# A fifth half-unit of weights in the opening block of each stage

## The chip, the cores and the metric

The kernel runs on one core of one Trainium2 chip. The metric is the device time of one execution in microseconds (us); a kernel's figure is the median of its runs. In the profile PE is TensorE (matmul), PEld its weight loads, DVE is VectorE, ACT is ScalarE, POOL is GpSimd and SP is SyncE, which issues the DMAs.

## What the kernel computes

Two layers act on 256 latent tokens and 256 context tokens of width 1024, with shared weights. Each layer is a half-step SwiGLU FFN, a mixing block, and a second half-step FFN. The core of the reference:

```python
for i in range(DEPTH):
    last = i == DEPTH - 1
    h = ffn_half_step(h, g_ffn1[i], m[0], m[1], m[2], w13_ffn1[i], w2_ffn1[i])
    hc = ffn_half_step(hc, g_ffn1[i], mc[0], mc[1], mc[2], w13_ffn1[i], w2_ffn1[i])
    n_lat = modulate(rms_norm(h, g_mix[i]), m[3], m[4])
    n_ctx = modulate(rms_norm(hc, g_mix[i]), mc[3], mc[4])
    z = n_lat @ w_in[i]
    zc = n_ctx @ (w_in[i][:, OFF_KV:OFF_G] if last else w_in[i])
    ...
    h = h + m[5] * y
    h = ffn_half_step(h, g_ffn2[i], m[6], m[7], m[8], w13_ffn2[i], w2_ffn2[i])
    if not last:
        ...                       # the same for hc
return rms_norm(h, g_final)
```

`ffn_half_step` is `h + 0.5 * gate * swiglu(modulate(rms_norm(h)))`. In the last layer the context is only needed for keys and values, so the last mixing block and the last FFN work mostly on the latent tokens alone.

## The kernel before, in words

**Data.** Activations lie feature-major: 8 chunks of 128 features by 512 columns, of which the first 256 are the latent tokens (half 0) and the next 256 the context tokens (half 1). Every float32 product is made of three matmuls in a reduced format (`mm3`, lines 191 to 193): high part of the weights times high part of the operand (`whi`, `nhi`), high times low (`whi`, `nlo`), and low times high (`wlo`, `nhi`).

**Weights.** They come as half-units: 128 output features by all 1024 inputs, 512 KB each. SP loads them in a fixed order into five staging tiles (`stg`). A conversion (`conv`, line 298) turns a staged half-unit into a pair of tiles: ScalarE copies the high part (`whi`, line 157) and then VectorE subtracts for the low part (`wlo`, line 165). For the second, third and fourth half-unit of each stage (the set `on_pool`) GpSimd makes the low part instead (line 303). There are five pairs (`HI = 5`). A half-unit that is finished (`done`, line 316) asks for the conversion of the one four places on (`AHEAD = 4`), so that at the opening of a stage four half-units are converted or under way and the fifth is not asked for until the first of the four is finished.

**Order.** A planner (`Weaver`) holds an estimate of TensorE's time. Side tasks (conversions, norms, evacuations) are generators that give the time at which they are next due; whenever the estimate passes a due time the task is resumed and emits its next instructions. This fixes the order on each engine's queue when the program is written. On the chip every engine works through its queue in that order and waits on semaphores.

**Changes of stage.** A stage ends with eight M-tiles in `final_half`, the last four of them half by half, latent half first. The norm of each half follows: sums of squares (ScalarE `sq`, GpSimd `acc`), a chain over TensorE, GpSimd and VectorE for the factor, and then `apply` (line 544) per chunk: `nt` on VectorE, `nhi` on ScalarE, `nlo` on VectorE. The next stage opens with `gemm_start` (line 604): four half-units, half by half, with the chunks k outermost and half-units in pairs (0, 1) and (2, 3), so that TensorE can start on chunk 0 while later chunks are still being normed.

`gemm_start` opens five stages: the first mixing block (stage M0, at 409 us of the span), the second FFN of layer 0 (F0, 573), the first FFN of layer 1 (F1, 946), the second mixing block (M1, 1322) and the last FFN (FL, 1419). It also opens the output projection inside each mixing block, which is not changed. FL is special ("raw"): the norm's factor is applied behind the product, and the operand of chunk k comes straight from the residual (`raw_in`, line 537). In M1 only half-units 2 and 3 have a context half; in FL none has.

**After the opening.** In an FFN the fifth half-unit is the first of the third pair (`pa`), made by `gemm` over all 512 columns. In a mixing block it is half of the gating input `u`, made by `gemm(i0 + 4, vs)`; after it come four (in M1 two) blocks of the gating input `vg` (lines 1309 to 1311), which use the sixth half-unit for chunks 0 to 3 and the seventh for chunks 4 to 7. When pair (2, 3) is done in a mixing block, `ev_kv` and `q_task` put the key, value and query work on VectorE and ScalarE.

Of the kernel before, what the change touches and what calls it, by code (L numbers as in the profile page):

```python
# [19 lines left out]
D = 1024  # L20
# [11 lines left out]

# columns of the per-layer parameter packs
PK1 = {}
# [19 lines left out]
class Weaver:  # L54
    """Keeps an estimate of TensorE's time and resumes side tasks when their turn comes."""

# [48 lines left out]
class Slots:  # L105
    """A fixed set of equal tiles, handed out in the order in which they came back."""

# [21 lines left out]
def block_kernel(ctx: ExitStack, tc: tile.TileContext, ins, out: bass.AP):  # L129
# [10 lines left out]

    # ---------------------------------------------------------------- pools
    cst = ctx.enter_context(tc.tile_pool(name="cst", bufs=1))
# [11 lines left out]

    # ---------------------------------------------------------------- engine helpers
    def act(o, i, func, after=0.0, n=None, **kw):
# [42 lines left out]

    # ---------------------------------------------------------------- the weight stream  # L200
    loads = []
# [121 lines left out]

    # ---------------------------------------------------------------- constants and residual
    ident = cst.tile([P, P], F32, name="ident")
# [40 lines left out]

    # ---------------------------------------------------------------- modulation
    mods, gains, gates, n_ada, n_mod = {}, {}, {}, {}, {}
# [14 lines left out]
    def gain_from(l, i, c0=0, c1=KC, n=2):  # L383
        """A = sqrt(D) g (1 + scale) for norm i."""
        m = mods[l][:, :n, (1, 4, 7)[i] * 8 + c0:(1, 4, 7)[i] * 8 + c1]
        vstt(gains[l][:, i, :n, c0:c1], m, 1.0,
             gains[l, "g"][:, i, None, c0:c1].to_broadcast([P, n, c1 - c0]), ALU.add, ALU.mult)
# [16 lines left out]
    def ada_quarter(q, tiles):  # L404
        """Layer 0's m0 and m1, column chunks 2q and 2q+1."""
        ps = yield from SM.get()
# [23 lines left out]
    def ada_tile(j, l, i):  # L430
        """128 columns of the modulation: VectorE's dot products of w_ada's columns with silu(c)."""
        r, c = i // KC, i % KC
# [20 lines left out]

    # ---------------------------------------------------------------- norms
    last = [False]
    acc, acc_i, acc_n, acc_t, last_sq = {}, {}, {}, {}, {}

    def square_in(v, c):
        """Adds the squares of h's chunk c, half v, to half v's sum."""
        if v not in acc:  # L460
# [19 lines left out]
    def sum_of(v):  # L480
        """Waits for half v's sum of squares; gives it with the time it is there."""
        while acc_n.get(v, 0) < KC:
            yield W.t + 50.0
        yield acc_t[v]
        acc_n[v] = 0
        return [acc.pop(v)] + ([last_sq.pop(v)] if v in last_sq else [])

    def rstd_chain(srcs, nblk, n_feat):
        """1/sqrt(sum + n eps) of the columns of src [128, 128 nblk], broadcast over partitions (in PSUM)."""
        ps = yield from SM.get()  # L490
        for b in range(nblk):
            for n, src in enumerate(srcs):
                t1 = mm(ps[:, b:b + 1], src[:, P * b:P * b + P], ones[:, :1], n == 0, n == len(srcs) - 1)
        yield from rstd_tail(ps, t1, nblk, n_feat)
        return ps
# [26 lines left out]

    # The last norm's factors are applied behind the first products: these take A h with the shift as one more column.
    raw_done = set()
# [19 lines left out]
    def apply(l, i, v, R, c0=0, c1=KC):  # L544
        """The modulated norm of h's chunks c0..c1, half v, as an exact sum of two float32r parts."""
        prev = None
# [28 lines left out]

    # ---------------------------------------------------------------- GEMM pieces
    hi_ = [0]
# [9 lines left out]
    def cols(ps, vs):  # L587
        """The columns of a PSUM tile that hold the halves vs."""
        return ps[:, vs[0] * T:(vs[-1] + 1) * T]

    def gemm(i, vs, nk=KC, xs=None, ps=None, ok=None, raw=False):
        """A feature-major tile: half-unit i against all k, halves vs."""
        ps = ps or ps_new()
# [10 lines left out]
    def gemm_start(i0, vss, evacs, ks=range(KC), ok=None, raw=False):  # L604
        """The four half-units at i0, half by half, k outermost, behind what makes their operand."""
        ok = ok or (lambda v, k: n_done.get(v, 0) > k)
        for j in range(4):
            conv_upto(i0 + j)
        pss = [ps_new() for _ in range(4)]
        for v in (0, 1):  # L610
            groups = [((0, 1), ks), ((2, 3), ks)]
            if not raw and 1 not in vss[3]:
                groups = [((0, 1, 2, 3), ks[:-2]), ((0, 1), ks[-2:]), ((2, 3), ks[-2:])]
            for js, k_part in groups:
                js = [j for j in js if v in vss[j]]
                if js:
                    for k in k_part:
                        W.until(lambda: ok(v, k))
                        xh, xl = raw_of(k) if raw else n_of(k, v)
                        for j in js:  # L620
                            wh, wl = wk(i0 + j, k)
                            mm3(pss[j][:, :T + 2] if raw else cols(pss[j], [v]), wh, wl, xh, xl, k == ks[0], k == ks[-1])
                for u in ((0, 1), (2, 3)):
                    if js and js[-1] == u[1] and k_part[-1] == ks[-1]:
                        if v == max(max(vss[u[0]]), max(vss[u[1]])):
                            for j in u:
                                done(i0 + j)
                            W.spawn(evacs[u[0] // 2](pss[u[0]], pss[u[1]]), W.t + 200.0)

    # ---------------------------------------------------------------- FFN  # L630
    def ffn(l, which, vs, tail):
        """h += 0.5 m (silu(a) b) w2 with a, b from the norm's output. Ends with the squares of the new h."""
        i_norm = (0, 2)[which - 1]
        full = len(vs) == 2
        with tc.tile_pool(name="ffn%d%d" % (l, which), bufs=2) as fp:
# [50 lines left out]
            for pi, (k0, k1_) in enumerate(PARTS):  # L686
# [3 lines left out]
                for m in range(k0, k1_):  # L690
# [3 lines left out]
                    if m == 0:  # L694
# [7 lines left out]
                        else:  # L702
                            gemm_start(i0, [vs] * 4, [evac(0, raw), evac(1, raw)],
                                       ok=(lambda v, k: k in raw_done) if raw else None, raw=raw)
                        hi_[0] += 4
# [43 lines left out]
    def final_half(vs, nk, xs, upd, tail, ok, raw=None):  # L749
        """The last eight M-tiles: the second four half by half, with h's squares and the norms behind them."""  # L750
        if xs:
# [29 lines left out]
    def fill():  # L781
        """Starts the modulation's tiles whose turn has come."""
        while ada_next[0] < len(ada_at):
# [15 lines left out]

    # ---------------------------------------------------------------- start  # L800
    def start_units(i0, evacs, fp, ST, GT):
        """The modulation's first columns, the first norm and the first half-units, in the order of arrival."""
        n_units = HI
# [47 lines left out]
        def chain(v):  # L851
            """The norm's factors of half v."""
            t = []
# [77 lines left out]

    # ---------------------------------------------------------------- mixing
    def mixing(l, tail):
# [4 lines left out]
        with ExitStack() as es:  # L938
# [23 lines left out]

            # -- blockdiag(C_c w_f), blockdiag(-S_c w_f)
            def bd_task():
# [13 lines left out]

            # -- q, k, v
            tb = Slots(W, mp, "tb", [P, 512], F32, TB)  # L980
# [106 lines left out]

            # -- attention
            def scores(v, hd, qb, pt):
                """exp of the scores, normalised and transposed into pt, for one block of queries."""  # L1090
                k0 = 0 if v == 0 else T
# [32 lines left out]
            def attention(v):  # L1124
                """All heads of half v's queries."""
                k0 = 0 if v == 0 else T
# [37 lines left out]

            # -- gating
            def y_of(g, j, v):
# [43 lines left out]

            # -- Fourier
            def fourier(v):
# [37 lines left out]

            # -- pooling
            def pooling(v):
# [30 lines left out]

            # -- the stream of projections
            gemm_start(i0, [vs, vs, [0, 1], [0, 1]], [ev_q, ev_kv])
            ps = gemm(i0 + 4, vs)
            done(i0 + 4)

# [54 lines left out]

    # ---------------------------------------------------------------- the two layers
    def norm_next(l, i):
# [34 lines left out]

# [1 line left out]
def _tiles(w):  # L1382
    """[K, M] -> [M/128, 128 (k in chunk), K/128, 128 (m)]"""
    k, m = w.shape
# [38 lines left out]
def _half_swap(w):  # L1423
    """Swaps the two halves of each rope axis in the last 32 columns' axis."""
    s = w.shape[:-1]
# [88 lines left out]
```

## Time and profile before

| | |
|---|---|
| median of 3 runs | 1625.59 us (1624.21 to 1625.91) |
| span of the profiled execution | 1622.2 us |
| granted TensorE clock, mean | 0.997 of full speed |
| TensorE busy | 1583.4 us, 98% of the span |
| VectorE busy | 1020.5 us, 63% |
| ScalarE busy | 556.9 us, 34% |
| GpSimd busy | 145.2 us, 9% |
| DMA | 245.53 MB, mean 151 GB/s |

The profile shows one execution. Its span goes from its first to its last instruction; the profile gives no other time for this execution, and the median of the runs is 3.4 us more than the span. Matmuls are pipelined and their ends are modelled, so that two matmuls overlap in the rows; time lost on TensorE is best read from start to start. An idle time in square brackets is followed by what ended it.

### The profile page before, as it was taken

Reading aid. Unit: us, or ns where it says so; the run is one execution under the profiler, and the core shown is the slowest. Engines: PE = TensorE matmul, PEld = TensorE weight load, DVE = VectorE, ACT = ScalarE, POOL = GpSimd, SP = SyncE. Lnnn points to the kernel's source line nnn. Section 1 sums busy time; section 2 is a strip of 40 time slices with the busy share of each in tenths; the row PEclk is TensorE's granted clock in tenths of the full one; section 3 lists DMA queues with packets and bytes.
Section 4 is the critical chain, followed back from the end, with each engine's and each line's share of the span. In section 5 each row is a group of like instructions: output and inputs, shape, how many; then the busy total and the mean of one; then the engine's idle time right before and its main releaser. Section 6 shows DMA issues by size and latency. Waiting matters only on the chain.

```text
span 1622.2 us, 22411 instructions
## 1 busy us (share of the span) xinstructions
PE 1583.4 (98%) x8862; PEld 1339.3 (83%) x8862; DVE 1020.5 (63%) x1693; ACT 556.9 (34%) x845; POOL 145.2 (9%) x115
## 2 busy tenths in 40 slices
PE   5999999999999999999999999999999999999997
PEld 3788888888867998888888898888888887899997
DVE  4568777877757476465563366776464367776674
ACT  3332221233534352222222243222222245554443
POOL 2000000004211320000000130000000051220001
PEclk9999999999999999999999999999999999999999
DMA  9355655654211144343352225566463222255452
GB/s 355 144 188 195 195 191 172 225 181 166 88 44 53 54 180 156 127 156 136 124 168 95 87 74 178 177 209 232 169 222 136 84 103 93 88 191 183 166 200 72
DMA packets 72057, 245.53 MB, mean 151 GB/s; under 512 B 8336, under 2 KB 10640, under 8 KB 71184
## 3 DMA queue, kind: packets, MB, share of 16 engines
q1 hardware_dynamic: 71664, 243.71, 44.0%
q8 instruction: 69, 1.13, 0.3%
q10 hardware_dynamic: 288, 0.39, 0.1%
q14 instruction: 36, 0.29, 0.1%
HBM read 243.03 MB, written 1.05 MB: 150 GB/s over the span
## 4 chain that ended last, share of the span: by engine, by line
PE 93%; DVE 5%; ACT 1%; issue 1%; DMA 0%; POOL 0%; SPq 0%; DVEq 0%; ACTq 0%; POOLq 0%
PE mm L191 28%; PE mm L193 28%; PE mm L192 28%; PE mm L184 5%; DVE nlo L169 2%; PE mm L197 1%; PE mm L1325 1%; PE mm L410 1%; DVE nt L169 1%; PE mm L1326 1%; PE mm L1327 1%; DVE wlo L165 0%; PE mm L1309 0%; PE mm L1310 0%; PE mm L1311 0%
## 5 line engine op out<-in xcount | busy, mean ns | idle before, releaser
L191 PE MATMUL mm<-nhi,whi 128*128 128x512 f32 (+2 forms) x1802 | 627.9, 348 | 3.1 <-ACT whi L157 3.1
L192 PE MATMUL mm<-nlo,whi 128*128 128x512 f32 (+2 forms) x1802 | 621.0, 345 | 10.1 <-DVE nlo L169 10.0
L193 PE MATMUL mm<-nhi,wlo 128*128 128x512 f32 (+2 forms) x1802 | 622.1, 345 | 1.0 <-DVE wlo L165 0.9
L157 ACT ACTIVATE whi<-stg 128x1024 fp32r<-128x1024 f32 (+1 forms) x310 | 318.1, 1032 | 434.8 <-PE mm L192 171.5
L165 DVE TENSOR_TENSOR wlo<-stg,whi 128x1024 fp32r<-128x1024 f32 (+1 forms) x288 | 347.7, 1211 | 89.2 <-ACT whi L157 88.7
L192 PEld LDWEIGHTS mm<-nlo,whi 128*128 128x128 f32 x1802 | 341.1, 189 | 58.7 <-DVE nlo L169 12.5
L191 PEld LDWEIGHTS mm<-nhi,whi 128*128 128x128 f32 x1802 | 340.6, 189 | 51.3 <-issue 4.4
L193 PEld LDWEIGHTS mm<-nhi,wlo 128*128 128x128 f32 x1802 | 340.5, 189 | 46.7 <-DVE wlo L165 1.7
L436 DVE SCALAR_TENSOR_TENSOR junk<-stg,sbc 128x1024 bf16<-128x1024 f32 x224 | 274.6, 1226 | 8.1 <-DMA stg<-in_w_ada 6.1
L191 PE MATMUL mm<-ghi,whi 128*128 128x512 f32 (+1 forms) x788 | 271.7, 345 | 0.0
L192 PE MATMUL mm<-glo,whi 128*128 128x512 f32 (+1 forms) x788 | 271.1, 344 | 0.0
L193 PE MATMUL mm<-ghi,wlo 128*128 128x512 f32 (+1 forms) x788 | 270.9, 344 | 0.0
L474 POOL TENSOR_TENSOR acc<-acc,sq 128x256 f32<-128x256 f32 x68 | 66.1, 978 | 1291.6 <-ACT sq L157 1123.7
L169 DVE SCALAR_TENSOR_TENSOR h<-mm,gates,h 128x256 f32<-128x256 f32 x168 | 75.6, 480 | 150.2 <-PE mm L193 150.2
L192 PEld LDWEIGHTS mm<-glo,whi 128*128 128x128 f32 x788 | 148.5, 188 | 19.6
L191 PEld LDWEIGHTS mm<-ghi,whi 128*128 128x128 f32 x788 | 148.6, 189 | 19.3
L193 PEld LDWEIGHTS mm<-ghi,wlo 128*128 128x128 f32 x788 | 148.3, 188 | 19.2
L165 DVE TENSOR_TENSOR g<-mm,s 128x512 f32<-128x512 f32 x66 | 45.6, 690 | 180.6 <-PE mm L193 179.9
L157 ACT ACTIVATE ghi<-g 128x512 fp32r<-128x512 f32 (+1 forms) x88 | 50.9, 579 | 286.7 <-DVE g L165 274.3
L157 ACT ACTIVATE nhi<-nt,mods 128x256 fp32r<-128x256 f32 x80 | 39.0, 506 | 84.1 <-DVE nt L169 84.0
L165 DVE TENSOR_TENSOR glo<-g,ghi 128x512 fp32r<-128x512 f32 (+1 forms) x88 | 54.5, 620 | 18.2 <-ACT ghi L157 18.2
L303 POOL TENSOR_TENSOR wlo<-stg,whi 128x1024 fp32r<-128x1024 f32 x22 | 55.7, 2535 | 61.7 <-ACT whi L157 61.2
(151 smaller groups left out, 854.3 us busy)
## 6 DMA issues: line engine op xcount, KB each, us to landing
stg<-in_w_ffn SPq DMA_DIRECT2D x208, 512.0 KB, 4.2
stg<-in_w_ada SPq DMA_DIRECT2D x128, 512.0 KB, 3.6
stg<-in_w_ffn SPq DMA_DIRECT2D x64, 448.0 KB, 3.1
stg<-in_w_in SPq DMA_DIRECT2D x22, 512.0 KB, 3.3
stg<-in_w_out SPq DMA_DIRECT2D x16, 512.0 KB, 3.4
sbc<-in_cb SPq DMA_DIRECT2D x3, 1024.0 KB, 7.0
pk<-in_pk SPq DMA_DIRECT2D x2, 1344.0 KB, 7.4
h<-in_xT SPq DMA_DIRECT2D x4, 512.0 KB, 6.0
```

The source lines that it names most:

```text
L157: nc.scalar.activation(o, i, func, **kw)
L165: nc.vector.tensor_tensor(out=o, in0=a, in1=b, op=op)
L169: nc.vector.scalar_tensor_tensor(out=o, in0=a, scalar=s, in1=b, op0=op0, op1=op1)
L184: nc.tensor.matmul(o, l, r, start=first, stop=last, skip_group_check=skip)
L191: nc.tensor.matmul(o, wh, xh, start=first, stop=False, skip_group_check=skip)
L192: nc.tensor.matmul(o, wh, xl, start=False, stop=False, skip_group_check=skip)
L193: nc.tensor.matmul(o, wl, xh, start=False, stop=last, skip_group_check=skip)
L197: nc.tensor.transpose(o, i, ident)
L303: nc.gpsimd.tensor_tensor(out=lo[:, :n], in0=raw, in1=hi[:, :n].bitcast(F32), op=ALU.subtract)
L410: nc.tensor.matmul(ps[32 * g:32 * g + 32, :P], sc[:, k], w[:, 128 * g:128 * g + 128], start=k == 0, stop=k == KC - 1)
L436: nc.vector.scalar_tensor_tensor(out=ada_tiles["junk"], in0=stage[j], scalar=1.0, in1=ada_tiles["s"][:, v], op0=ALU.mult, op1=ALU.mult, ac ...
L474: nc.gpsimd.tensor_tensor(out=acc[v], in0=acc[v], in1=s, op=ALU.add)
```

## The change

`gemm_start` takes a list of four or five half-units. The fifth gets a PSUM tile when its turn comes and its conversion is asked for at the entry of `gemm_start`. With five, the order is: latent half of (0, 1), of (2, 3), of the fifth; then the context half of the same. In FL the chunks are split as well: chunks 0 to 5 for (0, 1), (2, 3) and the fifth, then chunks 6 and 7 for the three. The FFNs hand the fifth's PSUM tile on through `early_a`, as the first stage does already; the mixing blocks use it for `u`. In the stages with two full halves the fifth half-unit is now 48 matmuls of 256 columns in place of 24 of 512. Comments and docstrings are dropped too.

```diff
     def gemm_start(i0, vss, evacs, ks=range(KC), ok=None, raw=False):
         ok = ok or (lambda v, k: n_done.get(v, 0) > k)
-        for j in range(4):
+        n = len(vss)
+        for j in range(n):
             conv_upto(i0 + j)
         pss = [ps_new() for _ in range(4)]
         for v in (0, 1):
-            groups = [((0, 1), ks), ((2, 3), ks)]
-            if not raw and 1 not in vss[3]:
+            groups = [((0, 1), ks), ((2, 3), ks)] + [((4,), ks)] * (n > 4)
+            if not raw and n == 4 and 1 not in vss[3]:
                 groups = [((0, 1, 2, 3), ks[:-2]), ((0, 1), ks[-2:]), ((2, 3), ks[-2:])]
+            elif raw and n > 4:
+                groups = [((0, 1), ks[:-2]), ((2, 3), ks[:-2]), ((4,), ks[:-2]),
+                          ((0, 1), ks[-2:]), ((2, 3), ks[-2:]), ((4,), ks[-2:])]
             for js, k_part in groups:
                 js = [j for j in js if v in vss[j]]
                 if js:
+                    if js[-1] == len(pss):
+                        pss.append(ps_new())
                     for k in k_part:
                         ...
-                for u in ((0, 1), (2, 3)):
-                    if js and js[-1] == u[1] and k_part[-1] == ks[-1]:
-                        if v == max(max(vss[u[0]]), max(vss[u[1]])):
+                for u in ((0, 1), (2, 3), (4,)):
+                    if js and js[-1] == u[-1] and k_part[-1] == ks[-1]:
+                        if v == max(max(vss[j]) for j in u):
                             for j in u:
                                 done(i0 + j)
-                            W.spawn(evacs[u[0] // 2](pss[u[0]], pss[u[1]]), W.t + 200.0)
+                            if len(u) == 2:
+                                W.spawn(evacs[u[0] // 2](pss[u[0]], pss[u[1]]), W.t + 200.0)
+        return pss[4] if n > 4 else None
...
-                            gemm_start(i0, [vs] * 4, [evac(0, raw), evac(1, raw)],
-                                       ok=(lambda v, k: k in raw_done) if raw else None, raw=raw)
+                            early_a.append(gemm_start(i0, [vs] * 5, [evac(0, raw), evac(1, raw)],
+                                                      ok=(lambda v, k: k in raw_done) if raw else None, raw=raw))
...
-            gemm_start(i0, [vs, vs, [0, 1], [0, 1]], [ev_q, ev_kv])
-            ps = gemm(i0 + 4, vs)
-            done(i0 + 4)
+            ps = gemm_start(i0, [vs, vs, [0, 1], [0, 1], vs], [ev_q, ev_kv])
```

## Rows read from the trace of the kernel before

**Rows 1.** The page: the span, and busy time of each engine.

```profile
span 1622.2 us, 22411 instructions
PE 1583.4 (98%) x8862; PEld 1339.3 (83%) x8862; DVE 1020.5 (63%) x1693; ACT 556.9 (34%) x845; POOL 145.2 (9%) x115
```

**Rows 2.** TensorE's waits, whole span: total us, times, longest us.

```profile
PE mm L192 <- DVE nlo L169: 10.0, 11, 1.6
```

**Rows 3.** Windows: length, then PE PEld DVE ACT POOL busy, PEclk, DMA.

```profile
409.00:417.00 8.00, 5.84 (x41) 4.99 (x41) 7.91 (x18) 3.69 (x7) 5.15 (x4) 1.00 0.25 81
424.00:436.00 12.00, 12.00 (x105) 12.00 (x104) 8.19 (x16) 9.76 (x19) 0.00 (x0) 1.00 0.22 69
...
952.00:956.00 4.00, 3.19 (x19) 3.08 (x20) 2.12 (x4) 0.51 (x1) 1.35 (x2) 0.80 0.35 131
956.00:960.00 4.00, 4.00 (x29) 4.00 (x28) 0.58 (x2) 0.00 (x0) 0.71 (x1) 0.77 0.00 0
...
1322.00:1330.00 8.00, 5.76 (x41) 4.91 (x40) 7.84 (x16) 3.94 (x8) 5.16 (x4) 1.00 0.27 92
...
1419.40:1428.20 8.80, 6.25 (x48) 5.62 (x47) 8.13 (x8) 4.54 (x8) 7.46 (x4) 1.00 0.43 149
```

**Rows 4.** Timeline at the opening of M0: start us, us, engine, line, operation.

```profile
412.94 2.59 POOL L303 TENSOR_TENSOR wlo<-stg,whi 128x1024 fp32r<-128x1024 f32 x1 [2.24 <-ACT whi L157]
...
413.62 2.19 DVE L169 SCALAR_TENSOR_TENSOR nlo<-nt,mods,nhi 128x256 fp32r<-128x256 f32 x1
...
415.48 0.92 POOL L474 TENSOR_TENSOR acc<-acc,sq 128x256 f32<-128x256 f32 x1
...
415.86 0.38 PE L192 MATMUL mm<-nlo,whi 128*128 128x256 f32 x1 [1.52 <-DVE nlo L169]
416.12 1.14 DVE L169 SCALAR_TENSOR_TENSOR nlo<-nt,mods,nhi 128x256 fp32r<-128x256 f32 x2
```

**Rows 5.** Timeline at the openings of F0, F1 and M1.

```profile
577.88 1.98 DVE L169 SCALAR_TENSOR_TENSOR nlo<-nt,mods,nhi 128x256 fp32r<-128x256 f32 x1 [0.57 <-ACT nhi L157]
...
952.82 0.39 PE L192 MATMUL mm<-nlo,whi 128*128 128x256 f32 x1 [1.64 <-DVE nlo L169]
953.08 1.14 DVE L169 SCALAR_TENSOR_TENSOR nlo<-nt,mods,nhi 128x256 fp32r<-128x256 f32 x2
...
1328.87 0.38 PE L192 MATMUL mm<-nlo,whi 128*128 128x256 f32 x1 [1.52 <-DVE nlo L169]
1329.13 1.14 DVE L169 SCALAR_TENSOR_TENSOR nlo<-nt,mods,nhi 128x256 fp32r<-128x256 f32 x2
```

**Rows 6.** Timeline of M1 where the blocks of vg begin.

```profile
1346.63 0.28 PE L1309 MATMUL mm<-whi,nhi 128*128 128x256 f32 x1
...
1347.50 2.34 DVE L165 TENSOR_TENSOR wlo<-stg,whi 128x1024 fp32r<-128x1024 f32 x2
...
1348.06 0.28 PE L1309 MATMUL mm<-whi,nhi 128*128 128x256 f32 x1
...
1348.77 0.39 PE L1310 MATMUL mm<-wlo,nhi 128*128 128x256 f32 x1 [0.43 <-DVE wlo L165]
```

**Rows 7.** Timeline of M0: the fifth half-unit, then the blocks of vg.

```profile
436.43 0.40 PE L191 MATMUL mm<-nhi,whi 128*128 128x512 f32 x1
...
441.11 2.35 DVE L165 TENSOR_TENSOR wlo<-stg,whi 128x1024 fp32r<-128x1024 f32 x2
...
442.00 0.28 PE L1309 MATMUL mm<-whi,nhi 128*128 128x256 f32 x1
```

**Rows 8.** Timeline at the opening of FL.

```profile
1424.27 2.58 POOL L303 TENSOR_TENSOR wlo<-stg,whi 128x1024 fp32r<-128x1024 f32 x1
...
1425.92 0.28 PE L191 MATMUL mm<-nhi,whi 128*128 128x258 f32 x1
1427.19 0.40 PE L192 MATMUL mm<-nlo,whi 128*128 128x258 f32 x1 [0.99 <-DVE nlo L169]
...
1428.35 1.06 ACT L157 ACTIVATE whi<-stg 128x1024 fp32r<-128x1024 f32 x1 [1.50 <-PE mm L192]
```

## The prediction

> **What bounds the kernel now.** I read the page first: TensorE is busy for 1583.4 of 1622.2 us [rows 1], so time can only be won or lost where TensorE waits. The list of its waits comes next: the largest is for `nlo`, the low part of a norm's output, 10.0 us in eleven waits [rows 2]. The windows then show where. In the first 8 us of M0 TensorE is busy for 5.84, in those of M1 for 5.76, in 8.8 us of FL for 6.25, while VectorE is busy almost throughout [rows 3]; F0 and F1 look alike. All of these waits lie in the latent half of the first pair, (0, 1). Where the context half runs, TensorE is busy for 12.00 of 12.00 us in M0 [rows 3], and it is full in the context halves of F0, F1 and M1 too. So the fifth half-unit's latent part, put ahead of the context half, hides no wait in M0, F0, F1 and M1: there is none to hide. This is the main reading. What is left to work out is what else the change moves.
>
> **Columns.** In M0, F0 and F1, 48 matmuls of 256 columns replace 24 of 512. The 24 take 442.00 - 436.43 = 5.57 us [rows 7]; twelve of 256 columns take 1348.06 - 1346.63 = 1.43 us [rows 6], 0.119 each, so 48 take 5.71. That is +0.14 three times: **+0.4 us** (0 to +0.6).
>
> **The fifth conversion comes earlier.** It was asked for when half-unit 0 was done, far behind the waits. It is now asked for at the entry, right behind the fourth's, so its `whi` stands on ScalarE behind the fourth's `whi`, and its `wlo`, on VectorE, one ScalarE conversion later, among the last `nlo` of the latent half. The planner's own costs give the place: in M0 it is due just ahead of chunk 6, in F1 and M1 between chunks 6 and 7, in F0 behind chunk 7. This is an order and no time, and in F1 and M1 it is close.
>
> First ScalarE. A `whi` of 1.06 us [rows 8] now stands ahead of `nhi` of chunk 5 and delays it to about 414.5. But the `nlo` that needs it starts at 413.62, lasts 2.19, and ends at 415.81, 0.28 after GpSimd's `wlo` (412.94 + 2.59 = 415.53) [rows 4]; the pair of `nlo` behind needs 1.14 for two. So it is held until GpSimd has finished, and a later start ends at the same time: 0 us. If the 2.19 were its own length, it would end 0.9 later; for four stages I keep 0 to +3.7. The Trainium skill has a rule for this ("SBUF — State Buffer", section "SBUF: two separate sides"): a VectorE operation with two inputs in SBUF and a GpSimd operation that reads SBUF exclude each other for the whole instruction. By that rule too the extra `whi` is free; without it the sum below would be 3.7 us higher.
>
> Then VectorE. Two `wlo` together take 2.35 [rows 7], 1.17 each, and nothing else covers them here. In M0 the pair of `nlo` for chunks 6 and 7 ends at 416.12 + 1.14 = 417.26 [rows 4]; with 1.17 ahead of both, chunk 6 is there at about 418.0, and TensorE, which got chunk 5 at 415.86 [rows 4] and needs 6 x 0.119 = 0.71 us and a restart for a chunk, wants it at 416.7: +1.3. In F1 chunk 5 comes at 952.82 and the pair ends at 954.22 [rows 5]; chunk 7 is wanted at 954.5 and is there at 955.4: +0.9. In M1 the same rows, 1328.87 and 1329.13 + 1.14 [rows 5], give +0.9. In F0 the last `nlo`, at 577.88 [rows 5], is ahead of the new `wlo`: 0. Together **+3.1 us** (0 if every `wlo` slips behind chunk 7; +5.2 if all four stages lose as M0).
>
> **The seventh half-unit comes late in the mixing blocks.** Its conversion is asked for when half-unit 2 is done. Before, the whole fifth half-unit lay between that and the blocks of `vg`, which want the seventh after four chunks of the sixth. Now all of it (M1) or half of it (M0) has gone ahead, while on VectorE the seventh's `wlo` still stands behind the key and query work that pair (2, 3) starts, its copies, products and sums. What is late next is thus a `wlo` in the middle of the block.
>
> M1: the fifth half-unit's 24 matmuls take 2.86 us and end at 1346.63 [rows 6], so pair (2, 3) ended at 1343.8. The seventh's `wlo` ends at 1347.50 + 1.17 = 1348.67, 4.9 us later; TensorE asks for it at 1348.18 and gets it at 1348.77 [rows 6], a loss of 0.59. After the change it asks 1.43 + 0.12 us after pair (2, 3), and the `wlo` comes 4.9 after it as before: a loss of 3.4, which is **+2.8 us**. M0: pair (2, 3) ends at 436.43, the seventh's `wlo` at 441.11 + 1.17 = 442.28 [rows 7], 5.85 later. TensorE will ask after 2.86 + 1.43 + 0.12 = 4.4: **+1.45 us**, where before it came after 7.1 and lost nothing. Queued behind the waiting matmul are the rest of `vg`, the last four half-units of the projection and the attention's matmuls; these slide with it. Bounds: 0 if the planner puts this `wlo` ahead of the key work; +6.4 if the attention slips by 2 us more behind it.
>
> **FL.** Here the order of chunks changes, and this is the one stage with something to win. TensorE waits at chunk 6 from 1425.92 to 1427.19 [rows 8], 1.15 more than a matmul's 0.12; with chunks 0 to 5 of the other half-units put there, the wait is gone. The earlier waits in FL, for chunk 3 and for the first `wlo`, stay: they come before chunk 6 in either order. But the fourth half-unit's `wlo`, on GpSimd, ends at 1424.27 + 2.58 = 1426.85 [rows 8], and is now wanted at 1425.92 + 5 x 0.119 = 1426.5: +0.35. And the sixth half-unit can only be converted when half-unit 0 is done and its pair free (the `whi` at 1428.35 waits for TensorE [rows 8]); that is now only 18 matmuls, 2.14 us, ahead of its use, and conversion takes 1.06 + 1.17 and two hand-offs: +0.2, or as much as +1.5 behind the evacuations. **-0.6 us** (-1.15 to +0.7).
>
> **Sum**, against the profiled execution: 0.4 + 3.1 + 2.8 + 1.45 - 0.6 = **+7.1 us**, a span of 1629.3. The runs' median is 3.4 above the span, and I add the difference to the median: 1625.59 + 7.1 = **1632.7 us**, +0.44%. About 0.2% (3.3 us) is what a measurement of this kernel can tell from no change.
>
> **Rivals.** *Not slower: the low parts stand elsewhere in VectorE's queue.* The plan is made anew from M0 on, and its due times are close. If the seventh's `wlo` goes ahead of the key and query work, it is ready before TensorE asks, and both mixing terms go; with the fifth's `wlo` behind chunk 7 in three stages too, 0.4 - 0.6 is left: 1625.4. It decides where each `wlo` stands against one neighbour. For it: in F1 and M1 the fifth's place is close. Against it: the seventh's is not, since the key and query work is due at once and the `wlo` one conversion later. *Partly so:* the mixing terms alone, 1629.6, still belong to the forecast.
>
> *Slower still: the clock.* In F1, just behind the waits, the granted clock falls to half: the mean is 0.80 and 0.77 in two windows of 4 us [rows 3], so (0.20 + 0.23) x 4 = 1.7 us are lost, 3.4 us at 1.2 in place of 2.4 GHz. M0, M1, F0 and FL wait as long and show no fall. With a single wait of 3.4 us in M1, and more in M0, a fall in both adds 3.4: 1636.1. The Trainium skill ("TensorE: Matmul & The Clock Gate", section "HAM oscillation — how this bites in real kernels") says that gaps on TensorE let the clock fall and are then paid for twice. By that rule alone every stage should have shown a fall; the trace shows one in five, so it has a small chance.
>
> *Faster.* The fall in F1 goes away with the new order (-1.7), FL wins its whole wait (-1.15), and no `wlo` is in the way: with +0.4, 1623.1, not yet 0.2%. It needs a wait that I took for fixed, such as chunk 3 in FL, to go as well. The change does what it says in every stage, so that it does nothing is no rival.
>
> **How the numbers follow.** The forecast, with both the early fifth and the late seventh, 0.56, its own range 1628.5 to 1635; the clock 0.14; not slower 0.21; faster 0.09. The predicted time is the forecast's, 1632.5. The range, 1625.2 to 1637, reaches over most of "not slower" and of the clock's case, and leaves out the faster case and the upper end of the bounds. Slower by over 0.2%: 0.56 + 0.14, less 0.03 for the forecast's lower end: 0.67. Within 0.2%: 0.24. Faster: 0.09.
>
> **What would show it.** In the changed kernel's trace: no wait of TensorE in the context half, as before; a `wlo` among the last `nlo` at the openings of M0, F1 and M1, and TensorE waiting about a microsecond more for `nlo` there; a wait for `wlo` at line 1310 of about 1.5 us in M0 and 3.4 in M1; in FL no wait at chunk 6 but short ones for `wlo`. The prediction is wrong if line 1310 doesn't wait, or if a fall of the clock comes or goes and outweighs the rest.

## The result, and the profile after

The changed kernel takes 1646.85 us (median of four runs, 1641.72 to 1647.20) against 1625.75 for the kernel before (four runs beside it): a ratio of 1.0125, 95% interval 1.0111 to 1.0139. That is slower, as forecast, but 21 us and not 7, and outside the range. The profiled execution is the shortest of the four, 1641.72 us with a span of 1639.9, 17.7 over the one before. The page, and TensorE's waits over the whole span (total us, times, longest), both of after:

```profile
span 1639.9 us, 22548 instructions
PE 1588.9 (97%) x8934; PEld 1344.9 (82%) x8934; DVE 1017.7 (62%) x1693; ACT 557.9 (34%) x845; POOL 144.9 (9%) x115
```

```profile
PE mm L192 <- DVE nlo L169: 8.0, 13, 1.1
...
PE mm L1317 <- DVE wlo L165: 4.9, 2, 3.5
PE mm L184 <- DVE dg L165: 4.8, 3, 1.7
...
PE mm L193 <- DVE wlo L165: 3.7, 3, 2.8
```

The waits for `nlo` are fewer microseconds than before [rows 2]. New are the waits for `wlo` at line 1317 (the old 1310) and one of 2.8 us for a `wlo` at line 193. The windows that answer to [rows 3], after:

```profile
408.50:416.50 8.00, 5.87 (x39) 4.72 (x37) 7.15 (x17) 4.53 (x8) 5.07 (x4) 1.00 0.27 88
424.00:436.00 12.00, 12.00 (x104) 12.00 (x103) 7.45 (x17) 5.61 (x10) 0.00 (x0) 1.00 0.01 1
...
1437.30:1446.10 8.80, 7.00 (x55) 6.38 (x54) 8.80 (x9) 4.40 (x7) 7.31 (x4) 1.00 0.47 153
```

M0's opening is as empty as before (5.87 of 8 us), its context half as full (12.00 of 12), and FL has gained 0.75 us of TensorE's time. Cutting both traces where TensorE begins the next stage gives the account, in us. FL is taken to the end of the span:

| stage | before | after | difference | predicted |
|---|---|---|---|---|
| start | 409.07 | 408.50 | -0.6 | 0 |
| M0 | 163.88 | 166.52 | +2.6 | +2.9 |
| F0 | 373.23 | 374.71 | +1.5 | +0.1 |
| F1 | 375.85 | 378.57 | +2.7 | +1.0 |
| M1 | 97.47 | 108.94 | +11.5 | +3.7 |
| FL | 202.73 | 202.66 | -0.1 | -0.6 |

The stretch ahead of M0 is the same code in every kernel here and took 408.4 to 409.4 us in their profiles. M0 and FL are about as predicted, F0 and F1 come out longer, and M1 is three times the forecast. First the opening of M0 (timeline, after), which answers to [rows 4]:

```profile
412.36 2.58 POOL L303 TENSOR_TENSOR wlo<-stg,whi 128x1024 fp32r<-128x1024 f32 x1 [2.24 <-ACT whi L157]
...
413.97 1.26 DVE L169 SCALAR_TENSOR_TENSOR nlo<-nt,mods,nhi 128x256 fp32r<-128x256 f32 x1 [0.85 <-ACT nhi L157]
...
415.54 1.36 DVE L165 TENSOR_TENSOR wlo<-stg,whi 128x1024 fp32r<-128x1024 f32 x1
...
416.82 0.87 DVE L169 SCALAR_TENSOR_TENSOR nlo<-nt,mods,nhi 128x256 fp32r<-128x256 f32 x2
417.35 0.38 PE L192 MATMUL mm<-nlo,whi 128*128 128x256 f32 x1 [1.09 <-DVE nlo L169]
```

The extra `whi` delays a `nhi`, and the `nlo` behind it now starts at 413.97 and ends 0.29 after GpSimd's `wlo`, as it did before by 0.28: free, as argued. The fifth's `wlo` stands at 415.54 ahead of the last pair of `nlo`, and TensorE waits 1.09 for it. Now M1 behind the second pair, which ends where `ta` is copied at 1353.83 (timeline, after), and below it the same chain before:

```profile
1353.83 0.42 DVE L180 COPY ta<-mm 64x256 f32<-64x256 f32 x1 [4.24 <-PE mm L193]
...
1357.61 3.48 DVE L165 TENSOR_TENSOR wlo<-stg,whi 128x1024 fp32r<-128x1024 f32 x3
...
1358.87 0.58 PE L1317 MATMUL mm<-wlo,nhi 128*128 128x256 f32 x1 [3.53 <-DVE wlo L165]
...
1367.07 0.16 DVE L174 TENSOR_SCALAR ss<-mm 128x2 f32<-128x2 f32 x1 [5.98 <-PE mm L184]
...
1370.11 5.06 POOL L303 TENSOR_TENSOR wlo<-stg,whi 128x1024 fp32r<-128x1024 f32 x2
1370.32 5.39 DVE L165 TENSOR_TENSOR dg<-ident,rs 128x256 f32<-128x256 f32 x2
...
1375.77 1.12 PE L184 MATMUL mm<-dg,ones 128*128 128x512 f32 x2 [1.72 <-DVE dg L165]
```

```profile
1343.98 0.42 DVE L180 COPY ta<-mm 64x256 f32<-64x256 f32 x1 [1.27 <-PE mm L193]
1351.07 0.16 DVE L174 TENSOR_SCALAR ss<-mm 128x2 f32<-128x2 f32 x1 [1.23 <-PE mm L184]
...
1353.19 0.42 DVE L165 TENSOR_TENSOR dg<-ident,rs 128x256 f32<-128x256 f32 x1
1354.17 0.69 DVE L165 TENSOR_TENSOR dg<-ident,rs 128x512 f32<-128x512 f32 x1 [0.56 <-POOL rs L502]
```

The wait for the seventh half-unit is there, 3.53 us for 3.4 forecast. But the reader should follow the key and query chain: from `ta` to its first sum (`ss`) it needed 7.1 us before and 13.2 after (the sum's matmuls stand behind the waiting one in TensorE's queue), and its two `dg`, 0.42 and 0.69 us before, take 5.39 together while GpSimd makes two `wlo` (5.06). This chain leads to the attention, and the projection behind the attention closes the stage.

### The profile page after: what moved, and what is told of

It is laid out like the page before. It is cut to its first block, busy times and chain, and to the rows that moved or that the text cites. A ratio compares the mean times of both kernels' runs of the same rounds, so it can differ in the third digit from the quotient of the medians.

```text
span 1639.9 us, 22548 instructions
## 1 busy us (share of the span) xinstructions
PE 1588.9 (97%) x8934; PEld 1344.9 (82%) x8934; DVE 1017.7 (62%) x1693; ACT 557.9 (34%) x845; POOL 144.9 (9%) x115
## 4 chain that ended last, share of the span: by engine, by line
PE 91%; DVE 5%; ACT 2%; issue 1%; POOL 1%; DMA 0%; SPq 0%; DVEq 0%; ACTq 0%; POOLq 0%
PE mm L191 28%; PE mm L193 27%; PE mm L192 27%; PE mm L184 4%; DVE nlo L169 2%; DVE wlo L165 1%; PE mm L1332 1%; DVE nt L169 1%; PE mm L1333 1%; PE mm L1334 1%; PE mm L197 1%; PE mm L410 1%; DVE dg L165 1%; ACT whi L157 0%; POOL wlo L303 0%
## 5 line engine op out<-in xcount | busy, mean ns | idle before, releaser
L192 PEld LDWEIGHTS mm<-nlo,whi 128*128 128x128 f32 x1826 | 345.7, 189 | 57.2 <-DVE nlo L169 10.9
L191 PEld LDWEIGHTS mm<-nhi,whi 128*128 128x128 f32 x1826 | 345.2, 189 | 53.3 <-issue 4.3
L193 PEld LDWEIGHTS mm<-nhi,wlo 128*128 128x128 f32 x1826 | 345.0, 189 | 45.9 <-DVE wlo L165 1.7
L157 ACT ACTIVATE s<-mm 128x512 f32<-128x512 f32 x66 | 38.7, 587 | 65.2 <-PE mm L193 65.2
```

Source lines behind the costliest of these rows:

```text
L157: nc.scalar.activation(o, i, func, **kw)
L191: nc.tensor.matmul(o, wh, xh, start=first, stop=False, skip_group_check=skip)
L192: nc.tensor.matmul(o, wh, xl, start=False, stop=False, skip_group_check=skip)
L193: nc.tensor.matmul(o, wl, xh, start=False, stop=last, skip_group_check=skip)
```

## The experiments

**Which stages.** Theory A: the mixing blocks carry the loss. Theory B: the planner's new plan costs something everywhere. Three kernels take the change in some stages only.

```diff
 # five_in_ffn and five_in_last: the mixing blocks as before
-            ps = gemm_start(i0, [vs, vs, [0, 1], [0, 1], vs], [ev_q, ev_kv])
+            gemm_start(i0, [vs, vs, [0, 1], [0, 1]], [ev_q, ev_kv])
+            ps = gemm(i0 + 4, vs)
+            done(i0 + 4)
 # the FFN openings: five is False in five_in_mix, and raw in five_in_last
+            p5 = gemm_start(i0, [vs] * (5 if five else 4), [evac(0, raw), evac(1, raw)],
+                            ok=(lambda v, k: k in raw_done) if raw else None, raw=raw)
```

> The fifth half-unit joins only in the two mixing blocks (M0, M1); the three FFN openings are as before. Theory A, the mixing blocks carry the loss: in the profile after, M1 is 11.2 us longer and M0 with its tail about 4, so +13 to +16 us over before (1639 to 1642), with a wait for wlo of about 3.5 us at the vg line in M1 and 1.5 in M0. Theory B, the loss comes from the whole plan being made anew, in any stage, with the mixing blocks no worse than others: +3 to +8 (1629 to 1634).

> The fifth half-unit joins only in the three FFN openings (F0, F1, FL); the mixing blocks are as before. Theory A: the FFN openings cost little; F1's late load in the products with w2 (2.9 us) may come along, FL gives back 0.7: 0 to +4 us (1625.5 to 1629.5), and no wait for wlo at the vg line. Theory B: +8 to +14 (1634 to 1640). If the plan's stages are independent, this and the run with the mixing blocks alone add up to the whole, +21 us.

> The fifth half-unit joins only in the last FFN (FL), where its chunks 0 to 5 stand ahead of chunks 6 and 7 of the others. By the working of the prediction -0.6 us, bounds -1.15 to +0.7: 1624.5 to 1626.3, no wait at chunk 6. Rival: FL's gain is eaten behind the opening (the sixth half-unit converted late): 0 to +1.

Measured: mixing blocks 1642.06 us (ratio 1.0104, 1.0089 to 1.0119), FFN openings 1629.13 (1.0022, 1.0013 to 1.0032), FL alone 1625.46 (1.0001, 0.9992 to 1.0011). The first two sum to +20.3 of the 21.1: the stages' losses are separate, and theory A holds, with the first time at the upper end of its range. M1 is 108.95 us in the first and 97.43 in the second. FL alone brings its first product with `w2` 0.75 us earlier (50.73 to 49.98 us behind FL's start), but from there to the end it takes 152.51 us where it took 152.00. Its last product with `w2` is still 0.76 us earlier (191.47 for 192.23), so the 0.5 us is lost behind that, where the last norm is. In the median there is no change.

**What makes M1 long.** My theory was the seventh's late `wlo`. Its rival, theory C: in M1 the fifth's latent part (2.86 us) now stands ahead of the second pair's context part, so the key and query work starts 2.86 later, and the work that covered it is already done. Two kernels: the seventh's conversion asked for when the first pair is done, and the fifth's products put back behind the second pair with its conversion left early.

```diff
                             for j in u:
                                 done(i0 + j)
+                            if ok5 and u == (0, 1):      # early_seventh, mixing blocks only
+                                conv_upto(i0 + 6)
```

```diff
-        for j in range(n):
+        for j in range(n + conv5):                       # m1_conv_only: conv5=True in M1
             conv_upto(i0 + j)
...
+                gemm_start(i0, [vs, vs, [0, 1], [0, 1]], [ev_q, ev_kv], conv5=True)
+                ps = gemm(i0 + 4, vs)
+                done(i0 + 4)
```

> The changed kernel, but in the mixing blocks the seventh half-unit's conversion is asked for when the first pair is done, not when half-unit 2 is done. Theory A, the late low part of the seventh is what delays M1: the wait at the vg line goes (3.7 us in M1, 1.55 in M0) and what slid behind it comes back too (about 6 us in M1): 1633 to 1637. Theory C, the key and query work starts 2.9 us later because the second pair now ends behind the fifth's latent part, and the attention sets the end of M1 anyway: the vg wait goes but comes back as waits for the key and query chain before the attention; M1 stays 8 to 11 us longer than before, 1641 to 1647.

> The changed kernel, but in M1 the fifth half-unit's products stand behind the second pair again, as in the kernel before; its conversion is still asked for at the entry. Theory C, M1 is long because the second pair now ends 2.9 us later behind the fifth's latent part, so that the key and query work starts later with nothing left to cover it: M1 goes back to 97.5 + 0.7 us and the whole to 1635 to 1637. Theory D, the early conversion alone upsets the order on VectorE and GpSimd: M1 stays over 103 us, the whole over 1640.

Measured: 1640.52 us (1.0092, 1.0075 to 1.0108) and 1633.85 (1.0054, 1.0039 to 1.0069), each a little under the range that theory C gave, and far from those of A and D. M1 in pieces, us, from first matmul to first matmul of the kind that follows:

| | opening | `vg` | last projection, attention | `w_out` | M1 |
|---|---|---|---|---|---|
| before | 24.61 | 7.73 | 30.22 | 34.91 | 97.47 |
| after | 25.32 | 10.82 | 35.55 | 37.25 | 108.94 |
| early_seventh | 25.32 | 5.70 | 39.28 | 35.59 | 105.89 |
| early7_low_on_dve | 25.45 | 5.70 | 36.81 | 35.59 | 103.55 |
| m1_half | 25.42 | 10.69 | 32.68 | 36.12 | 104.91 |
| m1_conv_only | 25.85 | 7.74 | 30.22 | 34.91 | 98.72 |

With the products back in their place, everything behind the opening is as before (72.87 us for 72.86). With the wait at the `vg` line taken away instead, `vg` runs without a stop, yet only 3.05 us of M1 come back and the waits reappear in front of the attention, as theory C said. So the place of the fifth's products is worth 10.75 us of M1 behind its opening, and the late `wlo` about 3 of these: only about, because in early_seventh's profile the granted clock is low for longer (0.61 and 0.71 in the two windows of 5 us from 1390 on) than in the first (0.72 in the one from 1359 on). In M0 the early seventh brings all back: from `vg` to F0 it takes 130.89 us, after 132.26, before 130.94.

**GpSimd's low parts.** early_seventh's timeline, then that of the kernel in which M1's two low parts of `w_out` go from GpSimd to VectorE:

```profile
1365.63 2.56 POOL L303 TENSOR_TENSOR wlo<-stg,whi 128x1024 fp32r<-128x1024 f32 x1
1365.85 3.23 DVE L165 TENSOR_TENSOR dg<-ident,rs 128x256 f32<-128x256 f32 x2
...
1382.14 2.35 POOL L303 TENSOR_TENSOR wlo<-stg,whi 128x1024 fp32r<-128x1024 f32 x1
...
1382.22 2.55 DVE L165 TENSOR_TENSOR q<-sq 32x256 f32<-32x256 f32 x1
```

```profile
1364.92 1.02 DVE L165 TENSOR_TENSOR dg<-ident,rs 128x256 f32<-128x256 f32 x2
...
1381.09 0.42 DVE L165 TENSOR_TENSOR q<-sq 32x256 f32<-32x256 f32 x1
...
1389.79 1.09 PE L184 MATMUL mm<-pk,vg 128*64 128x128 f32 x16 [3.04 <-ACT tb L157]
```

TensorE's waits of that second kernel in the whole of M1, without those for a norm's `nlo`, and the window behind its longest wait:

```profile
PE mm L184 <- ACT tb L157: 3.0, 1, 3.0
PE mm L191 <- ACT nhi L157: 1.5, 2, 1.0
PE mm L197 <- ACT pt L157: 0.4, 1, 0.4
```

```profile
1390.00:1395.00 5.00, 4.57 (x30) 3.79 (x27) 3.90 (x10) 2.74 (x7) 0.00 (x0) 0.68 0.00 0
```

```diff
-        on_pool |= {first[l, 1] + per + j for j in POOL_MIX}
+        on_pool |= {first[l, 1] + per + j for j in (POOL_MIX if l == 0 else (1, 2, 3))}
```

> The kernel with the seventh half-unit asked for early, and in M1 the two low parts of w_out that GpSimd makes go to VectorE. In its M1 a dg takes 2.62 us and a q 2.55 where they take 0.42 alone, each while GpSimd makes a wlo. If these two holds (2.2 and 2.1 us) delay the key and query chain and with it M1's end, M1 gets 3 to 4.3 us shorter: 1636 to 1638. If the chain has slack there, or the two wlo of 1.2 us on VectorE cost as much, within 1 us of 1640.5.

> The kernel before, with the same two low parts of w_out in M1 on VectorE. Its GpSimd holds a wlo (2.26 us) and another (1.54), no dg or q. If only holds on the key and query chain count, within 1 us of before (1625.5); if GpSimd's help counts by itself, 1 to 3 us slower.

Measured: 1637.26 us (1.0074, 1.0059 to 1.0089), M1 2.3 us shorter than in early_seventh where 3 to 4.3 were expected (the medians differ by 3.3), and for the control 1626.73 (1.0011, 1.0002 to 1.0021), 1.6 slower than before, with 73.80 us behind M1's opening for 72.86. The two `dg` go from 3.23 to 1.02 us and `q` from 2.55 to 0.42. So GpSimd's help is worth 1.6 us in the kernel before, where it meets no `dg` and no `q`, and costs here, where it meets both. The Trainium skill ("SBUF — State Buffer", section "SBUF: two separate sides") says that a VectorE operation with two inputs in SBUF and a GpSimd operation that reads SBUF lock each other out for a whole instruction. The rows agree: `dg` and `q` last about as long as the `wlo` beside them. In this kernel neither the wait at the `vg` line nor GpSimd's holds are left, and M1 still loses 5.2 us behind its opening. TensorE waits there for 4.4 us (3.04, 0.97 and 0.43; one of the two waits for `nhi` lies in the opening), where the kernel before waits once, for 0.43 [rows 6]. The fall of the clock behind the wait of 3.04 us (granted clock, the third number from the end, 0.68) makes 1.6 (0.32 x 5). So 2.86 us of lost cover bring about 4 us of waits and a fall; how these divide, and whether the 0.9 us that the two low parts cost in the control is among them, is not shown.

**The dose.** Half of the fifth's products ahead of the second pair's context part in M1, half behind it.

```diff
-            groups = [((0, 1), ks), ((2, 3), ks)] + [((4,), ks)] * (n > 4)
+            groups = [((0, 1), ks), ((2, 3), ks)] + [((4,), ks[:4] if half else ks)] * (n > 4)
...                                                  # and chunks 4 to 7 at the end of gemm_start
```

> The changed kernel, but in M1 only half of the fifth half-unit's products (chunks 0 to 3, 1.43 us) stand ahead of the second pair's context part, the other half behind it. Theory C, the loss in M1 goes with how much of the fifth stands ahead of the second pair: the wait at the vg line falls from 3.7 to about 2.2 us, the key chain starts 1.4 us earlier, and M1 lands about half way between the changed kernel's 108.9 us and the 98.7 with the fifth behind: 102 to 105, in all 1639 to 1643. Rival: one order of the queues against another decides, so that M1 is near one of the ends (under 100.5 or over 107).

Measured: 1640.95 us (1.0094, 1.0079 to 1.0109); M1 104.91 us, 61% of the way from 98.72 to 108.94, with a wait at the `vg` line of 1.9 for the 2.2 expected. The kernel before thus had next to no room: 1.4 us of work taken from behind the second pair already costs 6.6 us behind the opening. Not all of that is cover: a `dg` (2.91 us) and a `q` (2.48) meet GpSimd's `wlo` here too.

**F1's late load.** In F1's products with `w2` TensorE waits once, far from the opening (timeline, after):

```profile
1080.33 0.33 SPq L263 DMA_DIRECT2D stg<-in_w_ffn  x1
...
1083.78 1.06 ACT L157 ACTIVATE whi<-stg 128x1024 fp32r<-128x1024 f32 x1 [7.51 <-DMA stg<-in_w_ffn]
...
1085.82 2.35 DVE L165 TENSOR_TENSOR wlo<-stg,whi 128x1024 fp32r<-128x1024 f32 x2
...
1087.09 0.50 PE L193 MATMUL mm<-ghi,wlo 128*128 128x512 f32 x1 [2.78 <-DVE wlo L165]
```

The load was issued when VectorE's dot product (`junk`, 1079.08 + 1.22) had given back a staging tile, and it came too late. The modulation's set-up is started behind `gemm_start`, which now holds one half-unit more, so all dot products of the stage stand later.

```diff
-    def ada_setup(fp):
+    def ada_setup(fp, t=9000.0):
...
 # in gemm_start; mid starts the set-up with t=11900, in F0 and F1 only
+                    if v and mid and js[0] == 2:
+                        mid()
```

> The changed kernel, but in F0 and F1 the modulation's set-up is started ahead of the second pair's context part, so that its dot products have the same distance from the start of the stage as before. If the dot products' shift by one half-unit is what makes a load of F1 late (a wait of 2.9 us in its products with w2), the wait goes and the time is 2.5 to 3.5 us under the changed kernel's: about 1643.5. Rival: the wait comes from the order of the loads itself, and stays: 1646.5.

> The fifth half-unit joins in the FFN openings alone, with the modulation's set-up started early so that F1's load is not late. If each stage's loss is its own, F1's late load goes (3.2 us less than the FFN openings alone, 1629.1): 1625 to 1627, no change against before. Rival: without the mixing blocks' shift the load is late again or another is: 1628 to 1630.

Measured: 1641.45 us (1.0102, 1.0086 to 1.0117), 5.4 under the changed kernel, which is more than the 2.5 to 3.5 expected. The wait is gone, and F1 behind its opening takes 341.99 us in place of 345.18, which is 3.2. The profiles don't place the other 2 us between the medians; a fall of the clock behind the wait, as the next run shows one, would make most of them. In the FFN openings alone: 1624.88 us, ratio 0.9995 (0.9985 to 1.0004), no change. That is the best version with five half-units that I found; no kernel tried is measurably faster than the kernel before.

**The 5 us between runs.** Over all eight runs of the changed kernel two stand at 1641.7 and six between 1645.1 and 1647.2.

> The changed kernel once more. Its profiled run was 1641.7 us and its timed runs 1646.8 to 1647.2. In the profiled run the granted clock fell only in F0's opening, though M0's opening fell to half in all five other profiled kernels with its order. If falls of the clock (1.4 to 2.7 us each) make up the 5 us, this profile shows either more falls than the first and a time near 1645, or a few falls and a time near 1642; the stage durations outside the openings stay within 0.3 us.

This profile is of a run of 1645.13 us. Its openings have the clock of the first profile, so my guess at the place was wrong: F1 behind its opening is 1.4 us longer than in the first profile, and M1's part from `vg` to `w_out` 1.8. Windows of 5 us behind the waits of 2.8 us (F1), 3.5 and 1.5 (M1), after_again and then after:

```profile
1088.00:1093.00 5.00, 5.00 (x16) 3.93 (x15) 2.69 (x5) 1.06 (x1) 0.00 (x0) 0.66 0.75 242
1361.00:1366.00 5.00, 5.00 (x32) 5.00 (x31) 1.75 (x2) 2.39 (x3) 0.00 (x0) 0.66 0.80 260
1396.00:1401.00 5.00, 5.00 (x29) 4.04 (x26) 3.49 (x11) 1.42 (x5) 0.00 (x0) 0.66 0.00 0
```

```profile
1088.00:1093.00 5.00, 5.00 (x23) 4.04 (x22) 3.01 (x7) 1.06 (x1) 0.00 (x0) 1.00 0.85 266
1359.00:1364.00 5.00, 5.00 (x32) 5.00 (x33) 2.09 (x2) 2.11 (x3) 0.00 (x0) 0.72 0.71 256
1394.00:1399.00 5.00, 5.00 (x52) 4.25 (x47) 4.75 (x16) 2.82 (x7) 0.00 (x0) 1.00 0.00 0
```

The third number from the end, the granted clock, tells it: 0.66 over 5 us is 1.7 us lost to the lower level, 1.2 GHz. The first profile has one such fall here, the second three. So two more falls behind waits make up the 3.4 us between the two profiled runs. That the runs up to 1647.2 have still more falls is likely, but no profile shows one of them.

## Why the prediction was wrong

The direction was right, and so were most terms. The size of one term failed, a wait was not foreseen, and the clock added to both.

**The main reading held.** No context half had a wait to hide (12.00 of 12.00 us in M0 after), and the waits forecast at line 1310 came, 1.4 us in M0 and 3.53 in M1.

**Columns: +0.14 a stage predicted, +0.1 measured.** Where no clock falls, F0 takes 373.15 to 373.36 us in four profiles with the new order (m1_conv_only 31.23 + 341.99 = 373.22) and 373.09 to 373.23 in three with the old. That is the right size, and too small to be told for certain.

**The fifth's early conversion: right.** M0's opening is 1.32 longer (1.3 + 0.14 forecast), M1's 0.7 (0.9), F1's 0.8 (0.9 + 0.14; ffn_ada 33.26 + 341.98 against 26.90 + 347.57 in five_in_last, both without a fall), F0's none.

**The seventh late, M0: right.** A wait of 1.4 us and +1.3 from `vg` on, for +1.45; it vanishes with the earlier conversion.

**The seventh late, M1: this step failed.** It priced the wait, 3.4 us, and was right on it. It then said that the rest of `vg`, the projection and the attention's matmuls "slide with it", and gave +2.8. Its upper bound for both mixing blocks was +6.4 "if the attention slips by 2 us more" (2.8 + 1.45 + 2 is 6.25, and the predicted time of 1632.5 is 0.2 under its own sum; neither matters here). Measured behind M1's opening alone: +10.75. The step counted the fifth's 2.86 us as cover lost to the `wlo`, but not as cover lost to the key and query chain, which starts when the second pair ends and leads to the last work of the stage. That the place of these products makes the loss is shown: with them put back, M1 behind its opening takes 72.87 us for 72.86. The chain had no room for them: with the wait and GpSimd's holds taken away TensorE still waits 4.4 us where it waited 0.4. The wait itself, GpSimd's `wlo` that now meet `dg` and `q`, and falls of the clock come on top. The parts were taken away one after the other, and each profile has its own falls, so their sizes (3.05 for the wait, 2.3 to 2.5 for GpSimd, 5.2 for the rest) are rough and hold in that order only.

**FL: right at the opening (-0.75 for -0.6), nothing in the median.** Why 0.5 us is lost behind the last product was not tried. There is one thing more: FL's opening has a fall of the clock (1.5 us) in two of the three profiles that keep the old order there and in none of the ten with the new one. The median of FL alone (1.0001, 0.9992 to 1.0011) shows no gain from that, and its interval leaves room for 1.3 us.

**Not foreseen: F1's load,** 3.2 us, a hundred microseconds behind the edit, through the staging tiles that the dot products hold. The prediction looked for moved work at the openings and in the mixing blocks alone, and put everything behind an FFN's opening at nothing without a reason.

**The clock** was my rival with 0.14, and it came along with the forecast, not in its place. The wait in M1 was followed by a fall in all five profiles that have it (0.66 to 0.72 over about 5 us), M0's opening fell in six of the eight profiles with its new order and in none of the five with the old, at 1.4 to 2.7 us each. F0's +1.5 is such a fall too: where it has none, F0 takes what it took before. I gave the clock little because one of the five openings before showed a fall [rows 3]. That was one execution: over all profiles, the openings left in the old order have a fall in 8 of 21 cases, with no wait over 1.6 us. The Trainium skill ("TensorE: Matmul & The Clock Gate", section "HAM oscillation — how this bites in real kernels") says of long idle gaps that the work behind each starts at the lower clock, so that they are paid for twice. For the single wait in M1 that was the better guide. The prediction's remark that by this rule every stage should have shown a fall read it too widely, since the longest wait in an opening before was 1.6 us [rows 2]. That falls come behind such short waits too is what these runs show.

## What to carry to other kernels

Before work is moved ahead of something, ask not only whether it hides a wait there, but what it covered where it stood: list the chains that start behind it, and find the one that ends the stage. A wait's price is not its length when the chain behind it is what the stage ends with; the bound must then be the whole cover moved, the hold by other engines and the clock, not a small addition. And where queues are planned by an estimate of time, an edit shifts what is due long after it: search the whole trace after, not the edited block.

## What the runs showed of the hardware

A `dg` that takes 0.42 us alone took 2.63 beside GpSimd's 2.56 us `wlo` (after, the first of the two), so one GpSimd instruction held the chain for 2.2 us. In M0 the clock fell to its lower level in six of eight profiles though no single wait there was longer than 1.1 us (0.56, 0.35, 0.91 and 1.10 us, one behind the other), while the same opening before, with waits of 0.55 and 1.52 us, showed no fall in five. One of the six, five_in_mix:

```profile
414.00:424.00 10.00, 7.64 (x50) 7.03 (x49) 4.31 (x7) 1.47 (x4) 3.16 (x3) 0.83 0.35 105
```

Which executions fall is not fixed: two profiles of the changed kernel, 1641.72 and 1645.13 us, differ by two falls, and its runs go up to 1647.2.
